# Projecting the recurrent values of four heads at once: 512-column matmuls in the first head instead of 256-column matmuls in the first and third

## The chip, the cores and the metric

The kernel runs on one core of a Trainium2 chip. The metric is device microseconds of one execution, taken as the median of the runs. Besides the times there is one profiled execution, whose records give each engine's instructions: PE (TensorE matmuls) and PEld (TensorE weight loads), DVE (VectorE), ACT (ScalarE), POOL (GpSimd) and SP (SyncE, which issues most DMAs).

## The reference

One decoder layer on 2048 tokens of width 1024, in float32. The part that matters here is the recurrent head group (four heads, keys and values of 128 each). Its values `hi` are a plain projection of the normed input, 512 columns wide, 128 for each head:

```python
u = rmsnorm(h, norm_mix_w[l])
proj = u @ w_in[l]
hq, hf, hi, hg, att = jnp.split(proj, [...])      # queries, forget gates, values, output gates, attention
f = lb + (1.0 - lb) * jax.nn.sigmoid(hf)
k_hg = 1.0 - f
v_hg = hi.reshape(B, S, HG_HEADS, HG_DV)
o_hg = hgrn2_chunkwise(q_hg, k_hg, v_hg, log_f)   # S_t = diag(f_t) S_{t-1} + k_t v_t^T,  o_t = S_t^T q_t
o_hg = rmsnorm(o_hg, hg_norm_w[l]) * jax.nn.silu(hg)
...                                               # sliding-window attention with sinks on `att`
h = h + mix @ w_out[l]                            # then the gated MLP with a causal convolution, and a norm
```

## The kernel before

The sequence is worked in two halves of 1024 tokens (`hf` 0 and 1). Each half has a mixer stage (recurrent heads and attention), an output projection (`out_proj`), the MLP (`gate_up`, `down`), and then the next half begins.

Every float32 matrix is split into a high part rounded to the matmul's format and a low remainder, and a product is taken as three matmuls: high by high, high by low, low by high. `prep` loads 512 KB of weights into a `raw` buffer (a ring of three, `RAW`), rounds them on ACT (L190, tile `whi`) and takes the remainder on DVE (L191, tile `wlo`). The high and low parts normally live in rings of two buffers each (`hi` and `lo` of the pool `w`); with `slots=True` they take buffers of another ring, the eight buffers tagged `m`, which otherwise hold each head's queries and results (`slot`), the residual stream and intermediates of the MLP. X is the input of the half, as 8 tiles of high parts (`XH`) and 8 of low parts (`XL`), 128 x 1024 each.

In the mixer stage a head `h` does the following, as Python generators `hgrn` and `attend` that are advanced in turn by the main loop (L1195 to L1226): project the forget gate (PSUM tile `f`) and the query (`hq`) with `unit` (48 matmuls of 512 columns each); project an attention query (`q`); put a diagonal product (`pdiag`) into the score tile ST; run seven doubling levels (`plev`, with updates of Q, K, f and ST on DVE, and for the first five levels a small DMA `odd`); transpose K (`pkn`), make the state updates (`pu`, chained on DVE as `SS`, L651), project the output gate (`g`), make the outputs (`po`), norm and transpose them (`pot`). Beside it runs one attention head pair: scores `psc`, softmax, transposes `ppt`, outputs `poT`.

The recurrent values are projected in heads 0 and 2 by `project_v`, two heads at a time. Here X is the stationary operand (128 tokens at a time, `tt` from 0 to 7) and the weights move, 256 columns for two heads. For each `tt` the 8 parts of the contraction make 24 matmuls into half of a PSUM bank (tile `pvv`, L698 to L700), and ACT writes the two heads' 128 columns into `v` with the row's scale (L702). Two `prep` calls (2 x 512 KB) bring the weights of two heads. The value tiles are a ring of `VB` = 2 buffers: heads 2 and 3 write where heads 0 and 1 stood.

The order on each engine is not that of the program text alone. The kernel is built with `schedule_with_timeline_sim=True`: a planner goes through the program in order of priority, asks a simulated timeline which instructions are ready, and writes each engine's queue out in advance. On the chip each queue is then worked in that fixed order. So the matmuls of `pvv` are found mixed with those of `plev`, `po` and `pot`. Buffers of a ring are handed out as they come free, and an instruction that needs one waits for the last reader of the one it gets.

Of the kernel before, what the change touches and what calls it, by code (L numbers as in the profile page):

```python
# [8 lines left out]
F32 = mybir.dt.float32  # L9
# [3 lines left out]
AF = mybir.ActivationFunctionType  # L13
# [4 lines left out]
P = 128  # L18
D = 1024
KT = D // P  # L20
# [3 lines left out]
TT = HALF // P  # L24
NB = HALF // 512
HG = 4
# [13 lines left out]
NEG = -1.0e30  # L40
UT = 7
RAW = 3
VB = 2
KB = 2
WARM = 12
TAIL_WARM = 7
# [4 lines left out]
def hymba_layer(ctx: ExitStack, tc: tile.TileContext, a: dict, out: bass.AP):  # L51
    nc = tc.nc

    def pool(name, bufs=1, space=None, stack=ctx, **kw):
        if space is not None:
            kw["space"] = space
        return stack.enter_context(tc.tile_pool(name=name, bufs=bufs, **kw))
# [12 lines left out]
    def ps(kind, name):  # L70
        return spaces[kind].tile([P, 512], F32, tag=kind, name=name)
# [107 lines left out]
    def raw4(src):  # L179
        t = wp.tile([P, D], F32, tag="raw", name="raw", bufs=RAW)  # L180
        if src is not None:
            nc.sync.dma_start(t, src)
        return t

    def prep(src, slots=False):

        raw = raw4(src)
        hi, lo = [hp.tile([P, D], F32R, tag="m", name=f"w{t}", bufs=KT) if slots else
                  wp.tile([P, D], F32R, tag=t, name=f"w{t}", bufs=2) for t in ("hi", "lo")]
        nc.scalar.copy(hi, raw)  # L190
        nc.vector.tensor_tensor(lo, raw, hi.bitcast(F32), op=ALU.subtract)  # L191
        return hi, lo
# [206 lines left out]
    def att_keys(hf, kv, invb, p):  # L399

        KS = p.tile([P, 2, P + HALF], F32R, name="KS")
        V = p.tile([P, 1 + TT, P], F32, name="V")
        if hf:
            nc.vector.tensor_copy(KS[:, :, 0:P], kc)
            nc.vector.tensor_copy(V[:, 0], vc)
        kT, vT = [p.tile([P, HALF], F32, tag="t4", name=n, bufs=2) for n in ("kT", "vT")]
        for jj, dst in ((ATT_J, kT), (ATT_J + 1, vT)):  # L410
            o = kv[jj - ATT_J]
            for b, bs in halves():
                nc.vector.tensor_tensor(dst[:, bs], o[b], invb[:, bs], op=ALU.mult)
                nc.scalar.activation(dst[:, bs], dst[:, bs], AF.Identity, bias=C.battn[:, jj:jj + 1])
        for kv in range(2):
            r, other = rows(kv), rows(1 - kv)
            nc.scalar.copy(KS[r, kv, P:], kT[r])
            nc.vector.tensor_tensor(KS[other, kv, P:], kT[r], KS[r, kv, P:].bitcast(F32), op=ALU.subtract)
        for b in range(NB):
            pv = ps("at", "pv")  # L420
            for i in range(4):
                t0 = (b * 4 + i) * P
                nc.tensor.transpose(pv[:, i * P:(i + 1) * P], vT[:, t0:t0 + P], ident)
            nc.scalar.copy(V[:, 1 + 4 * b:5 + 4 * b].rearrange("p a b -> p (a b)"), pv)
        if hf + 1 < NH:
            nc.vector.tensor_copy(kc, KS[:, :, HALF:HALF + P])
            nc.vector.tensor_copy(vc, V[:, TT])
        return KS, V
# [258 lines left out]

    def project_v(hf, parts, X, rs, p):

        v = [p.tile([P, TT, P], F32, tag="v", name="v", bufs=VB) for _ in range(2)]  # L690
        for tt in range(TT):
            o = ps("mm", "pvv")
            t = slice(tt * P, (tt + 1) * P)
            for kt in range(KT):
                hi, lo = parts[kt // 4]
                xh, xl = X[kt]
                c = slice((kt % 4) * 256, (kt % 4 + 1) * 256)
                nc.tensor.matmul(o[:, 0:256], xh[:, t], hi[:, c], start=kt == 0, stop=False)  # L698
                nc.tensor.matmul(o[:, 0:256], xl[:, t], hi[:, c], start=False, stop=False)  # L699
                nc.tensor.matmul(o[:, 0:256], xh[:, t], lo[:, c], start=False, stop=kt == KT - 1)  # L700
            for i in range(2):
                nc.scalar.activation(v[i][:, tt], o[:, i * P:(i + 1) * P], AF.Identity, scale=rs[:, tt:tt + 1])  # L702
        return v

    def split_into(h, l, src, eng=None):
        return (nc.scalar.copy(h, src),  # L706
# [480 lines left out]
    for hf in range(NH):  # L1187
        X, kv, invb, rs, f0 = nxt
        with ExitStack() as st:
            p = pool(f"mix{hf}", stack=st, reuse_waits="tile")  # L1190
            KS, V = att_keys(hf, kv, invb, p)
            mix = [None] * KT
            vs = []
            M, WG = {}, {}
            for h in range(HG):  # L1195
                hg = hgrn(hf, h, X, invb, vs, WG, mix, p, f0 if h == 0 else None)
                at = attend(hf, h, X, invb, KS, V, mix, p)
                with tc.issue_after(summed.ins) if hf + h == 0 else ExitStack():
                    next(hg)
                if h == HG - 1:  # L1200
                    next(at)
                    next(hg)
                    for kt in (0, 4, 1, 5, 2, 6):
                        M[kt] = split(mix[kt])
                    next(hg)
                elif h % 2 == 0:
                    next(at)
                    wv = [prep(a["w_v"][h // 2, s]) for s in range(2)]
                    next(hg)
                    vs += project_v(hf, wv, X, rs, p)  # L1210
                else:
                    next(hg)
                    next(at)
                if h < HG - 1:
                    WG[h] = prep(a["w_g"][h])
                next(at)
                next(hg)
                if h < HG - 1:
                    next(hg)
                next(at)  # L1220
                if h < HG - 1:
                    next(at)
                    next(hg)
                else:
                    next(hg)
                    next(at)  # L1226
            M[7], M[3] = mix[7], mix[3]
        with ExitStack() as st:
            p = pool(f"ffn{hf}", stack=st, reuse_waits="tile")
            kept, ops, hs, first, last = out_proj(hf, M, p)  # L1230
            acts = gate_up(hf, ops, hs, first, last, p)
            nxt = down(hf, kept, acts, p)


def _layout(i):

    import numpy as np

    def cols(w, idx):
        t = w[:, idx].reshape(KT, P, len(idx))  # L1240
        return t.transpose(1, 0, 2).reshape(P, -1)

    x = i["x"][0]
    w_in = i["w_in"][0]
    ar = np.arange
    att0 = 2048
    att = [np.concatenate([att0 + j * HD + ar(HD), att0 + (j + 4) * HD + ar(HD)]) for j in range(4)]
    att += [att0 + 512 + ar(P), att0 + 640 + ar(P)]
    b = i["b_attn"][0]
    rows = [ar(P) + h * P for h in range(4)]  # L1250
    rows += [512 + np.concatenate([j * HD + ar(HD), (j + 4) * HD + ar(HD)]) for j in range(4)]
    w_out = i["w_out"][0][np.concatenate(rows)]
    w_v = np.stack([cols(w_in, 1024 + pr * 256 + ar(256)).reshape(P, 2, D).transpose(1, 0, 2) for pr in range(2)])
    conv = np.concatenate([i["conv_w"][0], i["conv_b"]], 0)
    d = {
        "xT": x.T.reshape(KT, P, S),
        "norm_mix_w": i["norm_mix_w"][0].reshape(KT, P).T,
        "w_q": np.stack([cols(w_in, h * P + ar(P)) for h in range(4)]),
        "w_f": np.stack([cols(w_in, 512 + h * P + ar(P)) for h in range(4)]),
        "w_v": w_v,  # L1260
        "w_g": np.stack([cols(w_in, 1536 + h * P + ar(P)) for h in range(4)]),
        "w_att": np.stack([cols(w_in, c) for c in att]),
        "b_attn": np.stack([b[c - att0] for c in att], 1),
        "lb_logits": i["lb_logits"].reshape(2, HG, P).transpose(2, 0, 1),
        "hg_norm_w": i["hg_norm_w"].reshape(P, 1),
        "sinks": i["sinks"].reshape(2, 4).T.reshape(1, 8),
        "w_out": np.stack([cols(w_out, t * P + ar(P)) for t in range(KT)]),
        "norm_ffn_w": i["norm_ffn_w"].reshape(KT, P).T,
        "final_norm_w": i["final_norm_w"].reshape(KT, P).T,
        "w_gate": np.stack([cols(i["w_gate"][0], t * P + ar(P)) for t in range(FT)]),  # L1270
        "w_up": np.stack([cols(i["w_up"][0], t * P + ar(P)) for t in range(FT)]),
        "conv": conv.reshape(4, FT, P).transpose(2, 1, 0),
    }

    w = i["w_down"][0].reshape(FT // 2, 2, P, 2, 4, P)
    d["w_down"] = w.transpose(3, 1, 2, 0, 4, 5).reshape(4, P, FT // 2, 512)
    return {k: np.ascontiguousarray(v) for k, v in d.items()}
# [16 lines left out]
```

## Time and profile before

| what | value |
|---|---|
| runs | 2198.18, 2198.51, 2198.69 us; median 2198.51 |
| profiled execution, span of its instructions | 2198.0 us |
| what lies around the span, against the median | 0.5 us |
| PE busy | 2180.4 us (99%), 11424 matmuls |
| weight loads busy | 1834.0 us (83%), 11424 |
| DVE busy | 1639.5 us (75%) |
| ACT busy | 1049.9 us (48%) |
| `pvv` matmuls | 768, at 70.0 to 98, 227 to 256, 1160 to 1188 and 1318 to 1347 us |
| mixer stage, first and second half | about 45 to 410 us, 1125 to 1500 us |

A row of a group gives busy time and the mean length of one instruction. Matmuls follow one another before the one ahead has ended, so the busy times of PE groups overlap and their sum is far over the span; the distance between two starts is read from the timeline.

### The profile page before, as it was taken

The numbers are of one execution on the slowest core, as the hardware profiler recorded it, in microseconds if no ns is written. First come the engines' busy times: TensorE is split into PE (matmuls) and PEld (weight loads), VectorE is DVE, ScalarE is ACT, GpSimd is POOL, SyncE is SP. The second block draws the span as 40 slices with busy tenths as digits, with TensorE's granted clock in tenths as the row PEclk, the third lists the DMA queues.
The fourth block names the chain that finished last, engine by engine and source line by source line (L and its number), as shares of the span: only waits on it lengthen the run. The fifth ranks groups of instructions, "written<-read, shape, count | busy, mean of one in ns | idle before, by whom it ended". The sixth has DMA issues, their size and how long they took to land.

```text
span 2198.0 us, 29524 instructions
## 1 busy us (share of the span) xinstructions
PE 2180.4 (99%) x11424; PEld 1834.0 (83%) x11424; DVE 1639.5 (75%) x2451; ACT 1049.9 (48%) x1848; POOL 6.3 (0%) x28
## 2 busy tenths in 40 slices
PE   9999999999999999999999999999999999999998
PEld 7988988888888888888889889888888888888888
DVE  6567568688887888885855666677888878887766
ACT  6445544454444445335735455544644444443353
POOL 1000000000000000000000000000000000000000
PEclk9999999999999999999999999999999999999999
DMA  4101112323333234964631111114132323259643
GB/s 155 51 32 48 39 41 68 119 74 102 104 109 108 89 127 143 372 241 156 209 125 41 44 36 51 58 39 134 58 125 92 125 91 109 98 183 393 233 144 130
DMA packets 94358, 257.91 MB, mean 117 GB/s; under 512 B 11594, under 2 KB 17546, under 8 KB 94218
## 3 DMA queue, kind: packets, MB, share of 16 engines
q1 hardware_dynamic: 88992, 251.30, 33.9%
q10 hardware_dynamic: 5226, 4.73, 0.7%
q8 instruction: 89, 1.46, 0.3%
q14 instruction: 51, 0.42, 0.1%
HBM read 195.10 MB, written 57.15 MB: 115 GB/s over the span
## 4 chain that ended last, share of the span: by engine, by line
PE 95%; DVE 3%; ACT 1%; DMA 1%; issue 0%; SPq 0%; DVEq 0%; ACTq 0%
PE X L877 7%; PE X L878 7%; PE X L879 7%; PE pop L212 7%; PE hq L212 4%; PE q L212 4%; PE f L212 4%; PE g L212 4%; PE Y L879 4%; PE Y L878 4%; PE Y L877 4%; PE pdx L1088 3%; PE pdx L1089 3%; PE pdx L1090 3%; PE pdy L1089 3%; PE pdy L1088 3%
## 5 line engine op out<-in xcount | busy, mean ns | idle before, releaser
L706 ACT CAST whi<-raw 128x1024 fp32r<-128x1024 f32 x88 | 92.6, 1053 | 109.2 <-PE X L878 68.2
L877 PE MATMUL X<-T,whi 128*128 128x512 f32 x352 | 136.9, 389 | 0.0
L878 PE MATMUL X<-T,whi 128*128 128x512 f32 x352 | 136.9, 389 | 0.0
L879 PE MATMUL X<-T,wlo 128*128 128x512 f32 x352 | 136.9, 389 | 0.0
L972 DVE SCALAR_TENSOR_TENSOR y<-ga,cw,y 128x1024 f32<-128x1024 f32 x88 | 112.5, 1281 | 26.0 <-ACT y L970 26.0
L884 ACT COPY u<-X 128x512 f32<-128x512 f32 x88 | 51.4, 585 | 133.3 <-PE X L879 133.1
L707 DVE TENSOR_TENSOR wlo<-raw,whi 128x1024 fp32r<-128x1024 f32 x88 | 107.3, 1220 | 0.0
L190 ACT CAST whi<-raw 128x1024 fp32r<-128x1024 f32 x57 | 59.5, 1048 | 93.1 <-PE q L212 31.9
L707 DVE TENSOR_TENSOR xld<-raw,xhd 128x1024 fp32r<-128x1024 f32 x72 | 80.8, 1133 | 19.1 <-ACT xhd L706 18.9
L706 ACT CAST xhd<-raw 128x1024 fp32r<-128x1024 f32 x72 | 69.7, 978 | 43.6 <-DMA raw<-act0T 14.8
L212 PE MATMUL pop<-XL,whi 128*128 128x512 f32 x256 | 86.1, 396 | 2.1 <-DVE XL L224 2.1
L212 PE MATMUL pop<-XH,wlo 128*128 128x512 f32 x256 | 85.2, 393 | 0.8 <-DVE wlo L191 0.8
L212 PE MATMUL pop<-XH,whi 128*128 128x512 f32 x256 | 84.5, 397 | 0.2
L878 PEld LDWEIGHTS X<-T,whi 128*128 128x128 f32 x352 | 66.1, 188 | 13.7
L877 PEld LDWEIGHTS X<-T,whi 128*128 128x128 f32 x352 | 66.1, 188 | 13.7
L879 PEld LDWEIGHTS X<-T,wlo 128*128 128x128 f32 x352 | 66.1, 188 | 13.7
L1088 PE MATMUL pdx<-xhd,hid 128*128 128x512 f32 x192 | 74.4, 391 | 1.0 <-ACT hid L706 1.0
L1089 PE MATMUL pdx<-xld,hid 128*128 128x512 f32 x192 | 74.7, 389 | 0.0
L1090 PE MATMUL pdx<-xhd,lod 128*128 128x512 f32 x192 | 73.7, 389 | 0.0
L698 PE MATMUL pvv<-whi,XH 128*128 128x256 f32 x256 | 73.5, 288 | 0.0
L191 DVE TENSOR_TENSOR wlo<-raw,whi 128x1024 fp32r<-128x1024 f32 x57 | 69.5, 1222 | 4.2 <-ACT whi L190 4.1
L699 PE MATMUL pvv<-whi,XL 128*128 128x256 f32 x256 | 72.6, 284 | 0.0
(379 smaller groups left out, 6563.3 us busy)
## 6 DMA issues: line engine op xcount, KB each, us to landing
wr<-in_w_down SPq DMA_DIRECT2D x90, 512.0 KB, 4.8
raw<-in_w_gate SPq DMA_DIRECT2D x44, 512.0 KB, 3.6
raw<-in_w_up SPq DMA_DIRECT2D x44, 512.0 KB, 3.6
raw<-act0T SPq DMA_DIRECT2D x20, 512.0 KB, 6.1
raw<-act1T SPq DMA_DIRECT2D x20, 512.0 KB, 10.1
act0B<-y SPq DMA_DIRECT2D x33, 256.0 KB, 2.6
act1B<-y SPq DMA_DIRECT2D x33, 256.0 KB, 2.4
raw<-in_w_out SPq DMA_DIRECT2D x16, 512.0 KB, 4.7
```

Of the source, the lines that this page charges most:

```text
L212: marks["unit"] = nc.tensor.matmul(o[b], w, x[:, bs], start=f, stop=l)
L698: nc.tensor.matmul(o[:, 0:256], xh[:, t], hi[:, c], start=kt == 0, stop=False)
L699: nc.tensor.matmul(o[:, 0:256], xl[:, t], hi[:, c], start=False, stop=False)
L706: return (nc.scalar.copy(h, src), (eng or nc.vector).tensor_tensor(l, src, h.bitcast(F32), op=ALU.subtract))
L707: (eng or nc.vector).tensor_tensor(l, src, h.bitcast(F32), op=ALU.subtract))
L877: nc.tensor.matmul(o, wh[:, ws], xh, start=i == 0 and not more, stop=False, skip_group_check=more)
L878: nc.tensor.matmul(o, wh[:, ws], xl, start=False, stop=False, skip_group_check=more)
L879: r = nc.tensor.matmul(o, wl[:, ws], xh, start=False, stop=i == 3, skip_group_check=more)
L972: nc.vector.scalar_tensor_tensor(y, g[:, w:w + HALF], C.cw[:, ft, w:w + 1], y, op0=ALU.mult, op1=ALU.add)
L1088: nc.tensor.matmul(o, wh[:, i, c], ah[:, i, cols], start=f, stop=False, skip_group_check=more)
L1089: nc.tensor.matmul(o, wh[:, i, c], al[:, i, cols], start=False, stop=False, skip_group_check=more)
L1090: nc.tensor.matmul(o, wl[:, i, c], ah[:, i, cols], start=False, stop=l, skip_group_check=more)
```

## The change

`project_v` is called once for each half, in head 0, for all four heads. Each matmul moves 512 columns and fills a whole PSUM bank; the number of `pvv` matmuls goes from 768 to 384, and each stationary tile of X is loaded half as often. ACT writes a whole bank with one instruction into a tile `v` that holds all four heads (16 KB in each partition; the ring of two had 8 KB). The four `prep` calls of a half stand together ahead of the projection in head 0: the first two use the `hi` and `lo` rings, the last two take four of the eight `m` buffers. Head 2 goes the way that head 1 goes. The weights are laid out in the host's arrangement as 4 parts of two contraction tiles with 512 columns each; their bytes are the same. The memory that the program sets aside for software DMA descriptors is set to 1024.

```diff
-VB = 2
...
     def project_v(hf, parts, X, rs, p):
-        v = [p.tile([P, TT, P], F32, tag="v", name="v", bufs=VB) for _ in range(2)]
+        v = p.tile([P, HG, TT, P], F32, name="v")
         for tt in range(TT):
             o = ps("mm", "pvv")
             t = slice(tt * P, (tt + 1) * P)
             for kt in range(KT):
-                hi, lo = parts[kt // 4]
+                hi, lo = parts[kt // 2]
                 xh, xl = X[kt]
-                c = slice((kt % 4) * 256, (kt % 4 + 1) * 256)
-                nc.tensor.matmul(o[:, 0:256], xh[:, t], hi[:, c], start=kt == 0, stop=False)
-                nc.tensor.matmul(o[:, 0:256], xl[:, t], hi[:, c], start=False, stop=False)
-                nc.tensor.matmul(o[:, 0:256], xh[:, t], lo[:, c], start=False, stop=kt == KT - 1)
-            for i in range(2):
-                nc.scalar.activation(v[i][:, tt], o[:, i * P:(i + 1) * P], AF.Identity, scale=rs[:, tt:tt + 1])
-        return v
+                c = slice((kt % 2) * 512, (kt % 2 + 1) * 512)
+                nc.tensor.matmul(o, xh[:, t], hi[:, c], start=kt == 0, stop=False)
+                nc.tensor.matmul(o, xl[:, t], hi[:, c], start=False, stop=False)
+                nc.tensor.matmul(o, xh[:, t], lo[:, c], start=False, stop=kt == KT - 1)
+            nc.scalar.activation(v[:, :, tt], o.rearrange("p (h d) -> p h d", h=HG), AF.Identity,
+                                 scale=rs[:, tt:tt + 1])
+        return [v[:, h] for h in range(HG)]
...
-                elif h % 2 == 0:
+                elif h == 0:
                     next(at)
-                    wv = [prep(a["w_v"][h // 2, s]) for s in range(2)]
+                    wv = [prep(a["w_v"][s], s > 1) for s in range(4)]
                     next(hg)
                     vs += project_v(hf, wv, X, rs, p)
...
-    nc = bacc.Bacc("TRN2", target_bir_lowering=False, num_devices=1)
+    nc = bacc.Bacc("TRN2", target_bir_lowering=False, num_devices=1, dynamic_dma_scratch_size=1024)
```

More of the change, by code (lines that the diff above doesn't have):

```diff
@@ L1252, in _layout @@
     w_out = i["w_out"][0][np.concatenate(rows)]
-    w_v = np.stack([cols(w_in, 1024 + pr * 256 + ar(256)).reshape(P, 2, D).transpose(1, 0, 2) for pr in range(2)])
+    w_v = cols(w_in, 1024 + ar(512)).reshape(P, 4, D).transpose(1, 0, 2)
     conv = np.concatenate([i["conv_w"][0], i["conv_b"]], 0)
```

## The prediction

> **What bounds the kernel now.** I read the page first: shares of the span, then the chain that ended last.
>
> ```profile
> PE 2180.4 (99%) x11424; PEld 1834.0 (83%) x11424; DVE 1639.5 (75%) x2451; ACT 1049.9 (48%) x1848; POOL 6.3 (0%) x28
> ...
> PE 95%; DVE 3%; ACT 1%; DMA 1%; issue 0%; SPq 0%; DVEq 0%; ACTq 0%
> ```
>
> PE idles for 2198.0 - 2180.4 = 17.6 us only, and 95% of the chain is PE. So what PE no longer has to stream is a gain one for one, as long as no new idle time takes its place. Then I asked how long the changed matmuls are. The grouped rows mislead here:
>
> ```profile
> L877 PE MATMUL X<-T,whi 128*128 128x512 f32 x352 | 136.9, 389 | 0.0
> L698 PE MATMUL pvv<-whi,XH 128*128 128x256 f32 x256 | 73.5, 288 | 0.0
> L699 PE MATMUL pvv<-whi,XL 128*128 128x256 f32 x256 | 72.6, 284 | 0.0
> L700 PE MATMUL pvv<-wlo,XH 128*128 128x256 f32 x256 | 72.1, 284 | 0.0
> ```
>
> By them 768 narrow matmuls take 73.5 + 72.6 + 72.1 = 218 us, and 384 wide ones at 389 ns 149 us: a gain of 69 us. But 288 and 389 ns are the lengths of single matmuls that overlap their neighbours. The price on a full engine is the distance of starts. I take it from two stretches of the timeline in which only one kind runs, with the count of each stretch from the table of windows:
>
> ```profile
> 237.73 0.28 PE L700 MATMUL pvv<-wlo,XH 128*128 128x256 f32 x1
> 237.85 0.28 PE L698 MATMUL pvv<-whi,XH 128*128 128x256 f32 x1
> ...
> 244.09 0.28 PE L699 MATMUL pvv<-whi,XL 128*128 128x256 f32 x1
> ```
> ```profile
> 599.82 0.39 PE L877 MATMUL X<-T,whi 128*128 128x512 f32 x1
> 600.05 0.39 PE L878 MATMUL X<-T,whi 128*128 128x512 f32 x1
> ...
> 613.88 0.39 PE L877 MATMUL X<-T,whi 128*128 128x512 f32 x1
> ```
> ```profile
> 237.80:244.20 6.40, 6.40 (x55) 6.40 (x55) 3.69 (x14) 1.37 (x6) 0.00 (x0) 1.00 0.00 0
> 600.00:614.00 14.00, 14.00 (x63) 11.59 (x63) 14.00 (x16) 8.37 (x11) 0.00 (x0) 1.00 0.13 39
> ```
>
> The columns are window, PE, PEld, DVE, ACT, POOL, clock and DMA, with (x) the instructions that overlap the window. The first stretch holds 54 `pvv` starts from 237.73 to 244.09 (the window's 55th is the one that was running when it opened), so 6.36 / 53 = 0.120 us from start to start. The second holds 63 from 599.82 to 613.88: 14.06 / 62 = 0.2268 us. In the narrow stretch PEld is busy without a gap (6.40 of 6.40), in the wide one for 11.59 of 14.00. So a narrow matmul is a little over half of a wide one, and no more.
>
> Last, the mixer stage by stretches: the narrow block of head 0, the rest of head 0, head 1, the block of head 2, the rest of head 2, and head 3 with the start of the output projection.
>
> ```profile
> 68.00:98.00 30.00, 30.00 (x280) 29.75 (x279) 19.64 (x36) 15.45 (x34) 0.00 (x0) 1.00 0.14 39
> 155.00:227.00 72.00, 72.00 (x468) 61.23 (x467) 48.28 (x94) 35.96 (x89) 0.00 (x0) 1.00 0.14 42
> 227.00:256.00 29.00, 29.00 (x246) 28.92 (x245) 14.03 (x28) 13.63 (x36) 0.00 (x0) 1.00 0.08 24
> 256.00:334.00 78.00, 78.00 (x487) 65.38 (x486) 53.40 (x98) 45.38 (x108) 0.00 (x0) 1.00 0.17 51
> 334.00:410.00 76.00, 73.34 (x492) 61.38 (x491) 57.78 (x117) 30.03 (x85) 0.00 (x0) 0.98 0.25 80
> 1424.00:1500.00 76.00, 73.52 (x497) 61.83 (x496) 57.39 (x115) 30.70 (x86) 0.00 (x0) 0.98 0.26 82
> ```
>
> PE is full everywhere but in the last stretch, which I call the tail: there it idles 2.66 us in the first half and 2.48 us in the second.
>
> **The change part by part.** *Matmuls.* 768 x 0.120 = 92.2 us go, 384 x 0.2268 = 87.1 us come: -5.1 us, 2.5 us in each half. The distances between blocks and the matmuls of `plev`, `po` and `pot` that lie in them I cost at nothing: these switches remain, in head 0 beside wide matmuls of `pvv`, in head 2 beside those of the next projections.
>
> The Trainium skill (TensorE: Matmul & The Clock Gate, Back-to-back issue gap) gives N/2.4 + 2.5 ns for N columns; that is 109 and 216 ns, and by it the sum would be -1.0 us, as an estimate. The rows above disagree with both figures, by 11 ns each, and the 11 ns count twice for the narrow pair.
>
> *Evictions.* 64 writes of 128x128 become 16 of 128x512.
>
> ```profile
> L702 ACT ACTIVATE v<-pvv,y 128x128 f32<-128x128 f32 x64 | 20.1, 365 | 40.8 <-PE pvv L700 36.5 <-DMA odd<-moved 1.5 <-PE po L665 1.4
> L884 ACT COPY u<-X 128x512 f32<-128x512 f32 x88 | 51.4, 585 | 133.3 <-PE X L879 133.1
> ```
>
> The new ones should last like L884's: 16 x 0.585 = 9.4 us in place of 20.1 us. ACT waits for PE here (36.5 us), so this is worth nothing on the path. A bank comes every 24 x 0.2268 = 5.4 us, and there are four, so 0.6 us of eviction holds nothing up.
>
> *The two preparations that are moved.* Each is a 512 KB load, a cast on ACT and a subtraction on DVE, now ahead of head 0's block instead of head 2's.
>
> ```profile
> 57.12 1.06 ACT L190 CAST whi<-raw 128x1024 fp32r<-128x1024 f32 x1 [4.01 <-PE hq L212]
> 68.00 1.05 ACT L190 CAST whi<-raw 128x1024 fp32r<-128x1024 f32 x1 [9.82 <-PE q L212]
> ...
> L191 DVE TENSOR_TENSOR wlo<-raw,whi 128x1024 fp32r<-128x1024 f32 x57 | 69.5, 1222 | 4.2 <-ACT whi L190 4.1
> ...
> L698 PE MATMUL pvv<-whi,XH x256: 277/283/384, 70.0 to 1347.1; 128*128 128x256 f32 x128
> ...
> 45.00:68.00 23.00, 23.00 (x106) 19.01 (x106) 8.55 (x12) 5.59 (x8) 0.00 (x0) 1.00 0.07 24
> ```
>
> The two casts shown are those of head 0, whose block starts at 70.0: each waits until the projection before it frees a ring buffer. The two new ones don't wait for that ring, since they take `m` buffers. ACT is busy for 5.59 and DVE for 8.55 of the 23 us ahead of the block, so 2 x 1.06 and 2 x 1.22 us fit there: cost nothing. If the queue puts them behind the cast at 68.00 instead, they end near 73 us, while the block would want its third part at 70 + 12 x 0.2268 = 72.7: a stall of up to about 1 us, or some 3 us if the fourth load has to wait for a `raw` buffer. So 0 to 3 us for each half, and I take 0.
>
> On SP's queue the two loads are moved past those that follow there:
>
> ```profile
> 26.49 5.57 SPq L182 DMA_DIRECT2D raw<-in_w_v  x2
> 33.09 0.33 SPq L182 DMA_DIRECT2D raw<-in_w_g  x1
> 59.80 0.33 SPq L182 DMA_DIRECT2D raw<-in_w_f  x1
> 70.68 0.33 SPq L182 DMA_DIRECT2D raw<-in_w_q  x1
> ...
> 96.98 1.05 ACT L190 CAST whi<-raw 128x1024 fp32r<-128x1024 f32 x1 [0.69 <-PE pvv L699]
> ```
>
> The output gate's weights were issued at 33.09 and first used at 96.98, so they can come some 40 us later and nobody waits; behind them stand only loads with as much time. POOL issues no loads, so the smaller software-descriptor memory delays none.
>
> *The longer block.* It grows from 192 matmuls in each head to 192 x 0.2268 = 43.5 us in head 0. Its first two weight buffers are held that long, and the cast of the output gate's weights (released by `pvv` in the row above) moves back with its end. Parts 0 and 1 are last read halfway through the last `tt`, 12 x 0.2268 = 2.7 us ahead of the end; a cast and a subtraction take 2.3 us. Hidden, with 0.4 us to spare, and state updates, outputs and scores of head 0 are there as cover.
>
> *What head 2 loses.* 192 x 0.120 = 23.0 us of PE work that lay beside DVE. Head 1, which has no block, runs with PE full (72.00 of 72.00) and DVE at 48.28 / 72 = 67%. From 227 to 410 us DVE is busy for 14.03 + 53.40 + 57.78 = 125.2 of 183 us. With two subtractions fewer that is 122.8 in 183 - 23 = 160 us: 77%, just the density of the tail (57.78 / 76 = 76%), where PE idles a little. So from below: the tail can gain what it now loses. Above: the 29.0 - 14.0 = 15.0 us in which DVE rests beside the block in each half come back as waits. I take no change, since head 1 is the nearest row and shows none.
>
> *Sum*: -5.1 us on PE, of which I strike 0.3 for switches between kinds: -4.8, and 0 for the rest. The profiled execution goes from 2198.0 to 2193.2; with the 0.5 us by which the median lies above it, **2193.7 us**.
>
> **The rivals.** *The tail falls behind (slower).* Head 2 without its block reaches head 3 with DVE's queue less far, and head 3's chain of levels, score updates and softmax sets the end. For it: DVE at 76% there already, PE idle 2.66 and 2.48 us. Against it: head 1's full PE, and that DVE rested for 13.7 us just ahead of the tail:
>
> ```profile
> 322.65 1.29 DVE L435 SCALAR_TENSOR_TENSOR att<-q,invb 128x512 f32<-128x512 f32 x2 [13.66 <-PE q L212]
> ```
>
> If half of the 15.0 us of lost rest comes back in each half, that is +15.0 - 4.8: 2208.7 us. It is even at 2.4 us of new idle time for each half, and measurably slower from 4.6. A measurement of this kernel tells about 0.2%, 4.4 us, from no change. A milder form, 0.5 to 4 us in each half, eats the gain: 2195 to 2202.
>
> *The tail improves.* The granted clock dips there:
>
> ```profile
> 360.00:370.00 10.00, 9.32 (x71) 8.07 (x71) 9.84 (x18) 2.49 (x14) 0.00 (x0) 0.91 0.00 0
> 370.00:380.00 10.00, 10.00 (x124) 8.36 (x120) 7.75 (x17) 2.18 (x5) 0.00 (x0) 0.92 0.01 2
> 1440.00:1450.00 10.00, 10.00 (x48) 8.43 (x49) 10.00 (x19) 5.02 (x19) 0.00 (x0) 0.83 0.36 107
> ```
>
> 10 x (0.09 + 0.08) = 1.7 us and 10 x 0.17 = 1.7 us are lost. With the dips gone and a third of the 5.1 us of idle time: -4.8 - 3.4 - 1.7 = -9.9, 2188.6 us. Another order of the tail could do that, or as well add a dip.
>
> *The change doesn't do what it says: a wide matmul costs two narrow ones* here (0.240 us), since X is stationary in this block. Then the time is that of before, 2198.5, whatever the formula. Against it: the wide rows show 0.2268 with a new load for each matmul.
>
> *Weight loads that don't overlap.* If each of the 384 loads saved were paid beside its matmul, at 0.107 us (16 one-column matmuls in the row below, (1.84 - 0.24) / 15), the gain would be 41 us: 2157.5.
>
> ```profile
> 31.01 1.84 PE L266 MATMUL pst<-ones,invb 128*128 128x1 f32 x16
> ```
>
> Against it: 0.120 us from start to start leaves 0.013 us for 256 columns. The Trainium skill states this rule (same page, The mechanism): a load overlaps running matmuls "only when row_grp differs". By that rule, the trace disagrees.
>
> **How the numbers follow.** Forecast, with the tail within 1 us for each half (2191.7 to 2195.7): 0.46; three fifths of it lie below 2194.1. Gain eaten by the tail or by late casts (2195 to 2202): 0.20. Tail falls behind: 0.13. Tail improves: 0.15. Two narrow for one wide: 0.05. Loads: 0.01. So faster by over 0.2%: 0.28 + 0.15 + 0.01 = 0.44; slower: 0.13; within: 0.43. The range leaves out the loads, the worse half of the falling tail and the best of the improving one: 2187 to 2204.
>
> **What would show it.** Right: 384 `pvv` matmuls 0.227 us apart, one block of 42 to 46 us in each half and none near 230, PE full in heads 0 to 2, tails with 2 to 3.5 us idle. The casts at the start: no PE gap at the first `tt`. Wrong: PE idle over 5 us in a tail, with DVE or ACT as what ended it; a gap ahead of `pvv` released by `wlo`; or wide `pvv` matmuls 0.24 us apart.

## The result: 37 us slower

The changed kernel takes 2235.6 us (2233.34 to 2236.85, five runs), the kernel before 2198.18 us (2198.05 to 2198.69, five runs): a ratio of 1.0169 with an interval of 1.0158 to 1.0179. The forecast was 2193.7 us in a range of 2187 to 2204, so the sign was wrong, and the time lies outside. Line numbers of the changed kernel are one lower from L43 on, and two lower at the eviction.

First the page of the changed kernel: span, engines, and shares of the chain that ended last.

```profile
span 2233.9 us, 28726 instructions
PE 2188.2 (98%) x11040; PEld 1826.2 (82%) x11040; DVE 1636.8 (73%) x2451; ACT 1045.4 (47%) x1804; POOL 6.5 (0%) x28
PE 96%; DVE 2%; ACT 1%; issue 0%; DMA 0%; SPq 0%; DVEq 0%; ACTq 0%
```

PE has 384 matmuls fewer, and yet, at a lower granted clock (0.988 against 0.997), it is busy for 7.8 us more; beside that it idles for 2233.9 - 2188.2 = 45.7 us, where it idled for 17.6. By the shares alone this is still a kernel that PE bounds.

The waits of PE in the changed kernel (who waited for whom, us in total, times, longest) and a few 10 us windows of it (columns as in the prediction) show where the idle time lies:

```profile
PE ppt L494 <- DVE y L175: 6.5, 1, 6.5
PE ppt L494 <- DVE sc L485: 6.0, 2, 5.5
PE poT L505 <- DVE pp L497: 4.5, 2, 3.5
PE plev L601 <- DVE K L609: 3.7, 3, 1.5
PE plev L606 <- DVE K L609: 3.5, 3, 1.5
PE pkn L639 <- DVE K L609: 3.3, 3, 1.5
PE plev L606 <- DVE f L615: 3.0, 2, 1.5
```
```profile
280.00:290.00 10.00, 6.38 (x48) 5.46 (x47) 10.00 (x21) 4.14 (x8) 0.00 (x0) 0.83 0.15 52
350.00:360.00 10.00, 5.59 (x36) 5.29 (x38) 9.66 (x29) 6.20 (x32) 0.00 (x0) 0.66 0.01 2
390.00:400.00 10.00, 5.57 (x61) 4.92 (x61) 4.87 (x10) 2.06 (x5) 0.00 (x0) 0.53 0.01 2
```

All of it is late: heads 2 and 3 wait for DVE, and in the same windows the granted clock falls to between 0.53 and 0.83. It is tempting to stop here: the tail got longer. It didn't, as the next two views show. They are the stretches of the changed kernel from head 0's block to the end of the output projection (cut at the start of the block, its end, and the starts of heads 1, 2 and 3), and the tile view of `pdiag` from 130 to 200 us, which holds the first step of head 1's recurrence:

```profile
70.00:120.00 50.00, 50.00 (x282) 41.74 (x281) 24.21 (x40) 18.25 (x31) 0.00 (x0) 1.00 0.15 45
120.00:176.00 56.00, 56.00 (x342) 47.30 (x341) 33.22 (x73) 29.21 (x81) 0.00 (x0) 1.00 0.14 44
176.00:277.00 101.00, 101.00 (x625) 86.29 (x624) 65.25 (x132) 55.79 (x141) 0.00 (x0) 1.00 0.14 40
277.00:361.00 84.00, 72.88 (x485) 62.08 (x484) 64.44 (x129) 47.75 (x125) 0.00 (x0) 0.94 0.19 58
361.00:476.00 115.00, 108.52 (x605) 91.37 (x605) 78.17 (x134) 44.64 (x84) 0.00 (x0) 0.96 0.26 85
```
```profile
L543 PE MATMUL pdiag<-hg,K x16: 270/275/275, 176.1 to 177.8; 128*128 128x128 f32 x16
```

The same row of the kernel before:

```profile
L544 PE MATMUL pdiag<-hg,K x16: 270/275/275, 155.3 to 157.0; 128*128 128x128 f32 x16
```

Head 1 begins 20.8 us later (176.1 against 155.3), in a stretch in which PE never idles and the clock is 1.00. From there to the start of the last matmul of the output projection it takes 300.3 us (to 476.4), and 303.9 us before (to 459.2). These two stretches, first in the kernel before, then in the changed one:

```profile
155.30:459.20 303.90, 301.24 (x1903) 257.44 (x1902) 212.50 (x396) 155.06 (x366) 0.00 (x0) 0.99 0.21 65
176.10:476.40 300.30, 282.69 (x1710) 239.99 (x1710) 208.25 (x394) 148.58 (x349) 0.00 (x0) 0.97 0.20 62
```

So two things make the result of a half: head 1 starts 20.8 us later, and the rest, from which 192 matmuls or 23.0 us of PE work have gone, is only 3.6 us shorter. Waits (PE idles for 17.6 us instead of 2.7) and a lower clock (0.97 instead of 0.99) have taken the place of that work. The second half shows the same: from the first `pdiag` of head 0 to that of head 1 it takes 108.4 us (87.3 before), and from there to the end of the output projection 300.2 us (303.8 before).

### The profile page after: what moved, and what is told of

Same layout as the page of the kernel before. It is cut to its first block, busy times and chain, and to the rows that moved or that the text cites. A ratio compares the mean times of both kernels' runs of the same rounds, so it can differ in the third digit from the quotient of the medians.

```text
span 2233.9 us, 28726 instructions
## 1 busy us (share of the span) xinstructions
PE 2188.2 (98%) x11040; PEld 1826.2 (82%) x11040; DVE 1636.8 (73%) x2451; ACT 1045.4 (47%) x1804; POOL 6.5 (0%) x28
## 4 chain that ended last, share of the span: by engine, by line
PE 96%; DVE 2%; ACT 1%; issue 0%; DMA 0%; SPq 0%; DVEq 0%; ACTq 0%
PE pop L211 7%; PE X L876 7%; PE X L877 7%; PE X L878 7%; PE hq L211 4%; PE f L211 4%; PE g L211 4%; PE q L211 4%; PE pdx L1087 4%; PE pdx L1089 4%; PE Y L878 4%; PE pdx L1088 4%; PE Y L877 4%; PE Y L876 4%; PE pdy L1089 3%; PE pdy L1087 3%
## 5 line engine op out<-in xcount | busy, mean ns | idle before, releaser
L608 DVE TENSOR_TENSOR Q<-Q,f 128x512 f32<-128x512 f32 x56 | 38.6, 690 | 96.7 <-PE plev L606 42.7
L876 PE MATMUL X<-T,Sh 128*128 128x512 f32 x176 | 68.7, 390 | 1.5 <-ACT s L883 1.5
```

The source lines that it names most:

```text
L876: nc.tensor.matmul(o, wh[:, ws], xh, start=i == 0 and not more, stop=False, skip_group_check=more)
```

## The experiments

"Start of head 1" is the first `pdiag` of that head in the first half, "end" the start of the last `pop` there, both from tile views. Ratios are to the kernel before, run on the same chip.

### The place or the width: four kernels

*The long block with narrow matmuls.* The changed kernel, but each `tt` in two passes of 256 columns:

```diff
+            for pr in range(2):
+                w = slice(pr * 256, (pr + 1) * 256)
...
-                nc.tensor.matmul(o, xh[:, t], hi[:, c], start=kt == 0, stop=False)
+                    nc.tensor.matmul(o[:, w], xh[:, t], hi[:, c], start=kt == 0, stop=False)
```

> The changed kernel, but with 256-column matmuls: the whole projection stays in head 0, in one bank per token tile, first the columns of heads 0 and 1, then those of heads 2 and 3. Theory A (place): what costs is that the values of heads 2 and 3 are projected ahead of head 1's gate and query, which delays every later head, and that head 2 loses the work that lay beside its chain. Then the time stays near the changed kernel's 2235.6 us, plus the 5.1 us of the narrow matmuls: 2232 to 2248. Theory B (width): the wide matmuls or the one wide eviction upset the planned order. Then it falls back to 2198 to 2205.

Measured: 2238.54 us, 1.0184 (1.0169 to 1.0199); head 1 starts at 178.1. The loss is there without a single wide matmul of `pvv`: it comes with the place.

*No block in head 2.* The kernel before, with heads 2 and 3 using the values of heads 0 and 1 (their own projection is left out):

```diff
-                elif h % 2 == 0:
+                elif h == 0:
...
-                    vs += project_v(hf, wv, X, rs, p)
+                    vs += 2 * project_v(hf, wv, X, rs, p)
```

> The kernel before without head 2's projection: heads 2 and 3 use the values of heads 0 and 1, so 384 narrow matmuls, four preparations and 32 evictions are left out. If PE's work is the bound, as I had it, 2 x 23 us go: about 2152 us. Theory A: the block was cover for a chain of about the same length; much of the 46 us comes back as PE idle time and a lower granted clock, 2175 to 2200, and PE idle rises from 17.6 us to over 30.

Measured: 2193.23 us, 0.9979 (0.9969 to 0.9989). 384 matmuls, by 0.120 us 46.1 us of PE work, bring 5.5 us. The waits of PE in this kernel:

```profile
PE ppt L495 <- DVE sc L486: 6.6, 2, 5.5
PE ppt L495 <- DVE y L176: 6.5, 1, 6.5
PE poT L506 <- DVE pp L498: 4.5, 2, 3.5
PE plev L602 <- DVE K L610: 3.7, 3, 1.5
PE plev L607 <- DVE K L610: 3.6, 3, 1.5
```

This is the list of the changed kernel, nearly to the tenth, and the clock is the same too (0.988), in a kernel that is faster than before. So these waits and the lost clock are what became of the 46.1 us: work that was there to fill the time has gone, and the time stays. They don't make a kernel slower than the one before; for that something has to be put in elsewhere.

*The memory alone.* The order of before, with the tile for four heads, the first pair's weights in `m` buffers, and the descriptor memory of the change:

```diff
-        v = [p.tile([P, TT, P], F32, tag="v", name="v", bufs=VB) for _ in range(2)]
+        v = [whole[:, 2 * pair + i] for i in range(2)]
...
-                    wv = [prep(a["w_v"][h // 2, s]) for s in range(2)]
+                    wv = [prep(a["w_v"][h // 2, s], h == 0) for s in range(2)]
```

> The kernel before with the memory of the changed one, all else as before: one value tile of 16 KB for the four heads, head 0's two preparations in the ring of eight buffers, descriptor memory at 1024. Theory A: 2196 to 2201, no change. Theory C (memory): if the buffers taken from the ring of eight or the descriptor memory hold something up, it is slower by a good part of the 37 us, 2210 or more.

Measured: 2198.8 us, 1.0002 (0.9992 to 1.0012). Buffers cost nothing. Head 1 starts at 166.0 us here, 10.7 later than before, but head 2 at 248.4 and head 3 at 343.5, as before (248.1 and 342.8). Head 1 isn't behind: 45 more matmuls stand ahead of its first `pdiag`, 26 of its own attention query and 19 of its own output gate (tile `g`), which stood behind it before, and 45 x 0.2268 = 10.2 us. So the start of head 1 marks where a half stands only as long as the same work stands ahead of it; where work has come forward, as here, a later start can cost nothing.

*Work put back into head 2.* The changed kernel, with 192 matmuls of 256 columns in each half where head 2's block stood; nobody reads their results:

```diff
+                elif h == 2:
+                    next(at)
+                    next(hg)
+                    unused(X)
```

> The changed kernel with 192 unused 256-column matmuls in each half, placed in head 2 where the second block stood (X by X, no weights, no evictions), and head 2 in the order that the kernel before has there. If PE is the bound, 2 x 23 us come on top: about 2282. Theory A: most of it falls into idle time of PE, and the clock stays up longer: 2230 to 2255.

Measured: 2241.28 us, 1.0202 (1.0185 to 1.0218). Its page, and its stretches from head 2 on:

```profile
span 2238.8 us, 29472 instructions
PE 2219.8 (99%) x11424; PEld 1858.5 (83%) x11424; DVE 1639.1 (73%) x2451; ACT 1045.5 (47%) x1802; POOL 6.0 (0%) x28
```
```profile
277.00:361.00 84.00, 84.00 (x528) 71.73 (x528) 57.74 (x112) 47.16 (x109) 0.00 (x0) 1.00 0.20 58
361.00:476.00 115.00, 112.11 (x665) 93.32 (x664) 88.52 (x157) 54.15 (x124) 0.00 (x0) 1.00 0.27 88
```

PE idles for 19.0 us as before (17.6), the clock is back at 0.998, and the time is not better but 5.7 us longer. Together:

| block in head 0 | with 23 us of PE work in head 2 | without |
|---|---|---|
| 192 narrow matmuls | 2198.7 (before) | 2193.2 |
| 192 wide matmuls | 2241.3 | 2235.6 (changed) |

Down a column the longer block costs 42.6 and 42.4 us, along a row head 2's work costs 5.5 and 5.7. The two add without touching each other, within the noise of the four medians (the interval of the kernel with work put back is 3.6 us to either side). The change is one step to the right and one down: -5.5 + 42.4 = +36.9. That the two steps give the whole is so by construction (37.4 in the result's own series); what the table shows is how unequal they are, and that neither depends on the other. The cells differ in a little more than their names say: the two kernels without the block have no preparations and evictions in head 2 either, and the work put back has none.

### Is it head 2's lost cover, or head 0's queue?

*The second pair in head 1.* Narrow, with the tile for four heads; head 2 loses its block, but head 0 keeps its length:

```diff
-                elif h % 2 == 0:
+                elif h < 2:
...
-                    vs += project_v(hf, wv, X, rs, p)
+                    vs += project_v(hf, wv, X, rs, whole, h)
```

> The kernel before, but the values of heads 2 and 3 are projected in head 1 instead of head 2, in narrow matmuls, into one value tile of 16 KB. Theory A: head 1's chain doesn't read these values, but its later steps queue behind them on PE; head 2 loses its cover as in the changed kernel. The block is not ahead of head 1's gate and query: so between, 2200 to 2225, with head 1's diagonal product at 155 us as before and head 2's later than 248. If the place didn't matter until head 0, 2196 to 2201; if the lost cover in head 2 is all, 2230 or more.

Measured: 2196.35 us, 0.9994 (0.9985 to 1.0004), clock 0.999, and not the 2200 to 2225 us of theory A. The second block lies from 163 to 192 us, and head 1 starts ahead of it at 161.7 (6.4 us later than before, with 26 matmuls of its attention query come forward). Had head 2 needed its own block as cover, this kernel would have been slow. Head 2 can do without it, if the work lies behind head 1's start; what is dear is work ahead of that start.

*The attention units moved back by one head*, on the changed kernel and on the kernel before (the same edit; head 0 then has no attention unit, head 2 has two):

```diff
-                at = attend(hf, h, X, invb, KS, V, mix, p)
+                ats = [attend(hf, j, X, invb, KS, V, mix, p) for j in ((), (0,), (1, 2), (3,))[h]]
```

> The changed kernel (wide block in head 0), with the attention heads run later: none in head 0, the first in head 1, the second and third in head 2, the fourth in head 3. An attention head has about 21 us of matmuls (query projection 10.9, scores, transposes and outputs the rest), as much as the block was lengthened. Theory A (head 0's PE work stands ahead of every later head, head 2's is cover): head 1's diagonal product comes back from 176 to about 155 us, PE idle to under 25 us, the time to 2190 to 2206. If something else in the longer block costs the 37 us, it stays above 2220.

> The kernel before with the same shift of attention, as a control. Theory A: head 0 gets about 20 us shorter, but head 2 now has two attention heads and the second block, 44 us of work beside a chain that needs about 20; PE was full, so at most a few us are won or lost: 2190 to 2215. If it wins as much as the shift wins in the changed kernel (over 25 us), the shift does something other than make up for the block.

Measured: 2208.68 us, 1.0047 (1.0032 to 1.0062), and 2212.87 us, 1.0071 (1.0054 to 1.0088). With attention's work out of its way head 1 starts at 157 us despite the long block, and 27 of the 37 us come back; the time is 2.7 us above the range that was expected, and PE idles for 28.5 us, not under 25. In this order the change is even a gain of 4.2 us (2208.68 against 2212.87). But both kernels are slower than the one before. That attention then crowds the late heads fits (head 3 of the shifted kernel before begins at 339 us, though its head 1 begins at 144), but no run tests it.

### Which queue: three kernels

Two ideas were left for why head 1 waits: that head 0's own steps need the whole block, or that PE's written order puts the block ahead of head 1's projections.

*Pair after pair.* Narrow blocks of two heads one behind the other in head 0, so that head 0's own values are ready after the first:

```diff
-                    vs += project_v(hf, wv, X, rs, p)
+                    for pr in range(2):
+                        vs += project_v(hf, wv[pr], X, rs, whole, pr)
```

> Both pairs projected in head 0 in narrow matmuls, as in the run with narrow matmuls there, but pair after pair: all eight token tiles of heads 0 and 1 first, then all eight of heads 2 and 3, so that head 0's values are complete after 28 us and not after 52. Theory A1 (a link): what counts is when head 0's own values are complete, since its state updates, outputs and head 1's levels follow from them; in the kernels so far head 1's diagonal product comes 56 us after the block's end. Then 2196 to 2210, with that product at 155 to 165 us. Theory A2 (a queue): any 20 us of matmuls ahead of head 1's gate and query count, whether or not they are read. Then 2230 or more, product near 176.

Measured: 2239.47 us, 1.0184 (1.0169 to 1.0199); head 1 at 178. Head 0's levels end at 102 us, but its next step, `pkn`, comes only at 124, behind the second pair that it doesn't need. So it doesn't help that head 0's own values are ready early: what counts is the order.

*The attention query behind the block*, in the changed kernel:

```diff
-                    next(at)
                     wv = [prep(a["w_v"][s], s > 1) for s in range(4)]
                     next(hg)
                     vs += project_v(hf, wv, X, rs, p)
+                    next(at)
```

> The changed kernel with the attention query of head 0 (10.9 us of matmuls) projected behind the wide block instead of ahead of it. Theory A1: the block starts at about 58 instead of 70 us and ends at about 109, so head 1's diagonal product comes at about 165 and the time falls by 2 x 11 us: 2208 to 2220. Theory A2: the same work stands ahead of head 1's projections in another order: 2230 to 2238.

Measured: 2233.86 us, 1.016 (1.0143 to 1.0177). The block begins at 57 us instead of 70, and head 1 still at 176: what was taken from in front of the block now stands behind it (the query's matmuls at 109 to 120 us), ahead of head 1.

*Attention units 0 and 1 both in head 1* (head 2 and 3 keep theirs):

```diff
+                ats = [attend(hf, j, X, invb, KS, V, mix, p) for j in ((), (0, 1), (2,), (3,))[h]]
```

> The changed kernel with the attention heads run later in another way: none in head 0, the first and the second in head 1, the third in head 2, the fourth in head 3. Head 0 loses about 21 us, as in the earlier shift, and head 1 takes them, where 23 us of the second block cost nothing. Theory A1: head 1's diagonal product at 155 to 160 us, head 3 as in the kernel before, time 2190 to 2202, so perhaps the first version with the wide block that is no slower. Against it: two attention heads in a row put about 28 us of DVE and ACT work into head 1, and the earlier shift lost 8 us in its tail.

Measured: 2222.73 us, 1.011 (1.0095 to 1.0125), against an expectation of 2190 to 2202. Head 1 does start at 157, but head 2 at 261 and head 3 at 352 (248 and 343 before): what head 0 got rid of came back in head 1. An early head 1 is not enough.

### Is it the length alone?

*Half of the wide block.* Of the 24 wide matmuls of each `tt` 12 are left out (the products with the low weights and half of those with the low input), so that the block is about as long as before:

```diff
-                nc.tensor.matmul(o, xl[:, t], hi[:, c], start=False, stop=False)
-                nc.tensor.matmul(o, xh[:, t], lo[:, c], start=False, stop=kt == KT - 1)
+                if kt % 2:
+                    nc.tensor.matmul(o, xl[:, t], hi[:, c], start=False, stop=kt == KT - 1)
```

> The changed kernel with half of the block's matmuls left out (the low part of the weights, and half of the products with the low part of X): 96 wide matmuls in each half, about 22 us, as long as the narrow block was. All else as in the changed kernel: wide matmuls, one wide eviction, four preparations, no block in head 2. Theory A2 (the length of what stands ahead of head 1's projections): head 1's diagonal product returns to about 155 us and the time to that of the kernel without head 2's block, 2188 to 2198. If preparations, evictions or the wide form matter, it stays 10 us or more above 2198.

Measured: 2213.46 us, 1.0074 (1.0058 to 1.0089), 15 us above the top of the expectation. By length it should have come out beside the kernel without a block in head 2 (2193.2); it is 20 us over it. The block does end at 95 us, but head 1 starts at 174.5. The tile view of `plev` from 60 to 130 us (min/median/max ns, first and last start) tells what else is late, here in this kernel, then in the kernel before:

```profile
L568 PE MATMUL plev<-Q,KK x40: 270/275/276, 75.7 to 102.0; 128*128 128x128 f32 x40
L606 PE MATMUL plev<-Q,K x48: 195/197/271, 107.3 to 114.7; 128*32 128x32 f32 x32, 128*64 128x64 f32 x16
```
```profile
L569 PE MATMUL plev<-Q,KK x40: 272/275/278, 73.6 to 91.0; 128*128 128x128 f32 x40
L607 PE MATMUL plev<-Q,K x48: 196/196/270, 94.4 to 99.9; 128*32 128x32 f32 x32, 128*64 128x64 f32 x16
```

Head 0's levels take 39 us instead of 26. PE's timeline shows why. Between the first two levels of the kernel before stand 27 narrow matmuls, in the changed kernel 23 wide ones (the `plev` rows are the levels themselves, the `pvv` rows the first matmul behind each):

```profile
73.64 1.07 PE L569 MATMUL plev<-Q,KK 128*128 128x128 f32 x8
...
77.78 1.07 PE L569 MATMUL plev<-Q,KK 128*128 128x128 f32 x8
```
```profile
75.86 1.07 PE L568 MATMUL plev<-Q,KK 128*128 128x128 f32 x8
76.68 0.48 PE L699 MATMUL pvv<-wlo,XH 128*128 128x512 f32 x1
...
82.03 1.07 PE L568 MATMUL plev<-Q,KK 128*128 128x128 f32 x8
82.85 0.48 PE L697 MATMUL pvv<-whi,XH 128*128 128x512 f32 x1
```

A level thus comes 6.2 us after the one before it instead of 4.1. The planner puts about the same number of matmuls between two levels wherever there are enough of them (23 also in head 1 of the kernel before, where they are wide ones of `q` and `g`), and the chip needs more time for wide ones. The same holds for the whole stretch: from 69 us to head 1's start I count 628 matmuls in the kernel before and 628 in the changed one, tile for tile the same list, and 626 here, where 94 of `g`, `q`, `f` and `psc` have come forward in place of the 96 that are gone. PE is busy for the whole stretch in all three, so head 1 starts when this list is done. Here that is 96 x 0.2268 = 21.8 us of the block and 82 x 0.2268 + 12 x 0.120 = 20.0 us of what came forward, in place of 23.0 us: 18.8 us more, and head 1 came 19.2 us later.

So two things go with a late head 1: a block that is long (narrow: levels done at 102, block at 122, head 1 at 178.1), or levels spread out by wide matmuls, between which later work is put (half the block: block done at 95, levels at 115, head 1 at 174.5). In the changed kernel both end together, levels at 114 and block at 120, head 1 at 176.1. The four preparations and the wide evictions don't spread the levels: the narrow block has both, and its levels are done at 102. That the spread is what costs the 20 us of half the block is a reading, though; no kernel changes it alone. What came forward there isn't lost, for the way from head 1 to the end takes 293.9 us instead of 300.0 in the kernel without head 2's block, but it makes up for 6 of the 19 us only.

*A try at a faster version:* the second pair, narrow, in head 1, and head 0's attention query behind its block:

```diff
+                elif h < 2:
+                    if h:
+                        next(at)
...
+                    vs += project_v(hf, wv, X, rs, whole, h)
+                    if not h:
+                        next(at)
```

> A try for a faster version: the narrow blocks in heads 0 and 1, as in the run that cost nothing, and head 0's attention query behind the first block, so that head 0's levels begin about 10 us sooner. Theory A2: the query stands ahead of head 1's projections either way, so the gain is small; PE was full until the tail, so at best some of its idle time goes: 2190 to 2200.

Measured: 2195.93 us, 0.9993 (0.9984 to 1.0001): no difference that can be told from the kernel before. No kernel here with the whole computation was measurably faster than it.

## Why the prediction was wrong, point by point

**The price of a matmul: right.** In the changed kernel 26 `pvv` matmuls start from 114.61 to 120.31 us, as these rows of the timeline begin and end:

```profile
114.61 0.39 PE L698 MATMUL pvv<-whi,XL 128*128 128x512 f32 x1
...
120.31 0.39 PE L699 MATMUL pvv<-wlo,XH 128*128 128x512 f32 x1
```

5.70 / 25 = 0.228 us, against 0.2268 in the forecast. The rival by which one wide costs two narrow ones fell with it. Of the 5.1 us that narrow and wide differ by, 2.9 show between the two long blocks (2238.54 and 2235.6), though their intervals overlap.

**Evictions, preparations, memory: right to cost them at nothing.** An eviction of 128x512 took longer than I thought, 0.688 us instead of 0.585, and lies beside PE's work:

```profile
L700 ACT ACTIVATE v<-pvv,y x16: 677/688/697, 80.1 to 1228.8; 128x512 f32<-128x512 f32 x16
```

PE is busy for 50.00 of 50.00 us from the block's start, so no cast came late; the memory by itself gave 1.0002.

**The longer block in head 0: the price was right.** Sorted by head, the sum has it with 41.0 us of PE work (384 x 0.2268 - 46.1); down the columns of the table it costs 42.6 and 42.4. In one half: the 628 matmuls ahead of head 1 are the same list as before, 192 of them take 0.107 us longer each, 192 x 0.107 = 20.5 us, and head 1 came 20.8 us later. "Hidden" was right for the buffers and casts that I asked about. I didn't ask what stands behind the block in PE's written order, which is the next head's start, and so took these 41 us for something that the other side of the sum would pay back.

**"What head 2 loses: I take no change": the step that failed.** The sum took 46.1 us off for head 2's block, one for one, with nothing for what the block covered. It brought 5.5 us; the other 40.6 came back, as idle time and lost clock. The bound that I set, 15.0 us for each half, was too low as well: 20.3 came back. Head 1's full PE was the row that I chose by, and it is no measure: PE is full there because later matmuls are at hand to be pulled forward. Take 46.1 us away, and the later work is pulled forward further and is missing at the end: without head 2's block the first matmul of the first half's output projection comes at 312.7 us instead of 334.2, and the last at 455.2 instead of 459.2. In the page of the kernel without head 2's block PE idles for 2189.5 - 2143.5 = 46.0 us, where it idled for 17.6:

```profile
span 2189.5 us, 28721 instructions
PE 2143.5 (98%) x11040; PEld 1798.5 (82%) x11040; DVE 1632.5 (75%) x2447; ACT 1040.1 (48%) x1816; POOL 6.5 (0%) x28
```

So the sentence "what PE no longer has to stream is a gain one for one, as long as no new idle time takes its place" failed by its condition. The Trainium skill (Perfetto Trace Analysis, Identifying the Most-Contended Engine) says to optimize the engine with the highest occupancy first, and for TensorE to judge the headroom by the matmul work done against the peak and by the weight loads' share, since busy matmuls mislead there. Busy time and load share both pointed at PE (99% and 83%), and the run without the block shows how little they tell for this stretch.

**The rival "the tail falls behind": its marks came, its reason only in part.** PE idles for more than 5 us late in the half, and DVE ends the waits. In the stretch from 343 to 459 us PE is busy for 113.34 us in the kernel before and for 102.38 in the changed one, whose half ends 17 us later:

```profile
343.00:459.00 116.00, 113.34 (x655) 94.10 (x655) 89.81 (x160) 54.71 (x124) 0.00 (x0) 0.99 0.27 89
343.00:459.00 116.00, 102.38 (x608) 87.06 (x608) 79.06 (x150) 48.66 (x122) 0.00 (x0) 0.93 0.23 74
```

But it isn't the rest that DVE had beside head 2's block, for with the second pair in head 1 that rest was gone too, and nothing was lost. What the traces show is that the way from head 1 to the end of the half takes 303.9 us before and 300.3 after, with 23.0 us of PE work in it or without. And it was priced at 15.0 us where 40.6 came.

**What stays open.** Why the planner writes the same number of matmuls whatever their width wasn't tried; its count fits a plan that prices them alike, and that is only argued. Nor is it settled what sets the pace from head 1 to head 3 (between 173 and 195 us in every kernel here, with 23 us of PE work in it or without), or how much of a late head 1 the later heads take up where work has come forward: all of 10.7 us in the kernel with the memory alone, which has head 2's block, but only a part of 19.2 us in the one with half of the wide block, which has none.

## What to carry to other kernels

An engine that is full in a stretch is not yet the bound: ask what would run there in the place of work that you take out, and what will then be missing at the end; one run that removes the work and one that adds it answer this. Where queues are written in advance, work put ahead of a chain's next start can cost its whole length (42.4 us for 41.0 here), and work behind it almost nothing (5.5 us for 46.1), so weigh the two sides of a move by their places and not by their length. Long instructions between the steps of a chain stretch each step (6.2 us for 4.1 here), even if their sum is no longer.

## What the hardware showed that was not expected

The granted clock falls behind a stretch in which PE rests, and can stay low while PE is already busy again. A row of PE's timeline and two windows of the changed kernel show one such place:

```profile
284.22 1.34 PE L505 MATMUL poT<-po,V 128*64 128x128 f32 x7 [3.52 <-DVE pp L497]
```
```profile
281.00:284.80 3.80, 0.48 (x4) 0.27 (x6) 3.80 (x7) 1.25 (x3) 0.00 (x0) 1.00 0.16 52
284.80:288.20 3.40, 3.40 (x27) 3.07 (x28) 3.40 (x9) 0.26 (x1) 0.00 (x0) 0.51 0.02 5
```

PE rests for 3.52 us, and the next 3.4 us run at half clock. The Trainium skill (TensorE: Matmul & The Clock Gate, HAM oscillation) warns of idle gaps over about 3.4 us, after which the clock is halved; with this row the trace agrees. As a bound the 3.4 us don't hold here, since shorter rests are followed by half clock too. First the kernel before, with one rest of 1.39 us, then the changed kernel, with one of four rests of 1.48 us each from 387 to 398 us:

```profile
1439.84 1.06 PE L212 MATMUL pop<-XL,whi 128*128 128x512 f32 x2 [1.39 <-DVE XL L224]
1440.00:1443.40 3.40, 3.40 (x9) 2.62 (x10) 3.40 (x7) 0.00 (x0) 0.00 (x0) 0.51 0.69 164
388.44 1.97 PE L601 MATMUL plev<-Q,K 128*128 128x64 f32 x16 [1.48 <-DVE K L609]
390.70:400.90 10.20, 6.06 (x61) 5.55 (x62) 4.62 (x10) 2.47 (x5) 0.00 (x0) 0.50 0.01 2
```

Nor does each such rest cost clock: a rest of 1.39 us that ends at 1479.0 us in the kernel with work put back is followed by 5 us at 1.00. What sets the bound stays open.

What the warning leads one to do here, keeping PE busy, is the kernel with work put back into head 2: the clock came back to 0.998, and the time did not. In the changed kernel the lost clock came with the work that had run out, and to bring it back with more work gained nothing.
